# Last token group of a GLA + SwiGLU block: its operand differences moved from the seam into the SwiGLU stage

## The chip, the cores and the metric

The kernel runs on one NeuronCore of a Trainium2 chip. The metric is the device time of one execution in microseconds (us). The kernel before took 2386.27 us (median of three runs, 2382.10 to 2387.61).

## The reference

One layer: a modulated, normalised gated-linear-attention (GLA) mixer over 2048 latent tokens (256 context tokens only start its states), then a modulated, normalised SwiGLU feed-forward layer with F = 2816 hidden units, all in float32. With D = 1024, cut to what matters:

```python
h_lat = modulate(rms_norm(lat, norm_g[i, 0]), mod_l[:, 0], mod_l[:, 1])
y_lat, y_ctx = gla_mixer(h_lat, h_ctx, ...)
lat = lat + mod_l[:, 2] * rms_norm(y_lat, norm_g[i, 1])
h = modulate(rms_norm(lat, norm_g[i, 2]), mod_l[:, 3], mod_l[:, 4])
gate, up = jnp.split(h @ ffn_w_in[i], 2, axis=-1)
lat = lat + mod_l[:, 5] * rms_norm((silu(gate) * up) @ ffn_w_out[i], norm_g[i, 3])
```

## The kernel before, in words

Every float32 product is made of three TensorE (PE) matmuls in the fp32r type: an operand is split into a high part (a cast on ACT) and a low part (a subtraction on DVE), and hi x hi, hi x lo and lo x hi are added up in PSUM (`mm3`, `product`).

The 2048 tokens are four groups g = 0 to 3 of 512. The first stage projects the groups and runs the forward scan. The second (`back`, steps b0 to b4) goes through the sixteen 128-token tiles from the last to the first: inter-chunk part, head norm, gate, projection with `wout` (the `py` matmuls), residual and norm. b4 makes the tile `y` = l1 (the residual stream, stored to `l1_d`), and `norm_tile` its normalised copy `xh`.

The SwiGLU matmuls use a seven-product scheme on 2x2 blocks (Strassen-Winograd, P1 to P7) instead of eight products. Its four token-side blocks are the upper and lower half of the features k of two groups: groups 2 and 3 form the pair p = 1, groups 0 and 1 the pair p = 0. For each pair, seven operands `T_d[p][P1..P7]` are written to HBM: three are raw blocks of h (P1 = b11 and P2 = b21 from the odd group, P3 = b22 from the even one), four are differences. `h2_units(g)` makes them. For an odd group, `first(k)` transposes four `xh` tiles on PE (`tp`), evicts and modulates them on ACT (`hf`, line 103) and stores h. For an even group, `second(k)` loads back b11 and b21 of the odd group, makes b12 and b22, and computes four differences per k (`comb`, line 781), on POOL for g = 2 and on DVE for g = 0; each is stored by the SP queue.

The third stage works on the pair p = 1 first, then p = 0. `load_T` loads an operand (four tiles of 256 KB for k = 0 to 3, line 860) and splits it (cast line 861, subtraction line 862). `Feat` loads the weights of one 128-row feature block (`wg`, 512 KB, line 894; two `wu` of 256 KB, line 897). `product(i)` splits the weight block (`whl`: cast line 924, subtraction line 925) and issues 12 matmuls (line 942). There are 44 steps t of seven products; a step takes P1, P2, P6 and P7 of its own block and P5, P4 and P3 of the block before. Beside them run `w2_units`, one unit per step: loads of `w2` (tag `wl`), differences on DVE (line 878), stores on POOL's queue. The results are combined by DVE and stored by POOL (line 970). The fourth stage multiplies by `ffn_w_out`.

The order on each engine is set by the tile framework's scheduler from the written order, its cost estimates and the buffers; each engine and each queue then runs its list in order, and a DMA issue that waits holds everything behind it on its queue. Memory is given to pools as a stack from the left and one from the right; a tile of a new pool waits for the old tiles whose place it takes. At the seam between stages two and three, the code closes the pools of stage two, runs what is left of `h2_units(0)` (`pend`), opens the pools of stage three and loads the operands of pair 1 in the order P1, P2, P6, P7, P5, P4, P3, and only then the first weights.

Of the kernel before, what the change touches and what calls it, by code (L numbers as in the profile page):

```python
# [7 lines left out]
F32 = mybir.dt.float32  # L8
# [3 lines left out]
ALU = mybir.AluOpType  # L12
PSUM = bass.MemoryType.PSUM
# [21 lines left out]
def trunk(ctx, tc, x, cx, modw, cols, rows, consts, wqkr, wv, wvg, wgate, wout, w1, w2, out):  # L35
    nc = tc.nc
    sync = nc.sync
    st = nc.sync
# [8 lines left out]
    T_d = [[dram.tile([4, 128, GT], F32, name=f"T_d{p}{i}") for i in range(7)] for p in range(2)]  # L47
# [602 lines left out]
    def back(gc):  # L650
# [91 lines left out]
        def b4(xhs):  # L742
            y, ss2, pys = e["y"], e["ss2"], e["py"]
            xt = sq.tile([128, D], F32, name="xt2", tag="xt2", bufs=2)
            sync.dma_start(out=xt, in_=x[128 * gc:128 * gc + 128, :])
            sst = sq.tile([128, 1], F32, name="sst", tag="sst", bufs=2)
            nc.gpsimd.tensor_tensor(out=sst, in0=ss2[:, 0:1], in1=ss2[:, 1:2], op=ALU.add)
            rs = rstd_of(sq, sst, 1, float(D), "y")
            for n in range(2):
                ns = slice(512 * n, 512 * n + 512)  # L750
                nc.vector.scalar_tensor_tensor(out=y[:, ns], in0=pys[n], scalar=rs[:, 0:1], in1=A2[:, ns],
                                               op0=ALU.mult, op1=ALU.mult)
            (nc.vector if gc == 0 else nc.gpsimd).tensor_tensor(out=y, in0=y, in1=xt, op=ALU.add)  # L753
            st.dma_start(out=l1_d[gc], in_=y)
            xhs.append(norm_tile(sq, y, "b"))

        return [b0, b1, b2, b3, b4, rload]

    def h2_units(g, xhs):
        p, n1 = divmod(g, 2)  # L760
        Td = T_d[p]

        def hmod(k):
            hf = sq.tile([128, GT], F32, name="hf2", tag="hf2", bufs=4)
            transp_mod(ps2, "pa", 4, xhs, k, hf, mcol[:, 2, 1, k:k + 1], mcol[:, 2, 0, k:k + 1])
            return hf

        def first(k):
            st.dma_start(out=Td[P1 if k < 4 else P2][k % 4], in_=hmod(k))

        def second(k):
            eng = nc.gpsimd if g else nc.vector
            bl = sq.tile([128, D], F32, name="bl", tag="xt2", bufs=2)
            b11, b21 = bl[:, 0:GT], bl[:, GT:D]
            sync.dma_start(out=b11, in_=Td[P1][k])
            sync.dma_start(out=b21, in_=Td[P2][k])
            b12, b22 = hmod(k), hmod(k + 4)
            st.dma_start(out=Td[P3][k], in_=b22)

            def comb(i, out, x, y):  # L780
                eng.tensor_tensor(out=out, in0=x, in1=y, op=ALU.subtract)
# [39 lines left out]
    pend = []  # L821
# [20 lines left out]

    p3 = ExitStack()
    hL = p3.enter_context(tc.tile_pool(name="hL", bufs=1, reuse_waits="tile"))
    w3 = p3.enter_context(tc.tile_pool(name="w3", bufs=2, reuse_waits="tile"))
    o3 = p3.enter_context(tc.tile_pool(name="o3", bufs=2, reuse_waits="tile"))
    ps3 = p3.enter_context(tc.tile_pool(name="ps3", bufs=1, space=PSUM, reuse_waits="tile"))
    for u in pend:
        u()
    p2t.close()  # L850
    hR = p3.enter_context(tc.tile_pool(name="hR", bufs=1, reuse_waits="tile", side="right"))
    ps3z = p3.enter_context(tc.tile_pool(name="ps3z", bufs=1, space=PSUM, reuse_waits="tile", side="right"))
    T = {}

    def load_T(p, i):
        pool = hL if i in (P1, P2, P6) else hR
        t = pool.tile([128, 4, 2, GT], F32R, name=f"T{i}", tag=f"T{i}", bufs=1)
        for k in range(4):
            raw = t[:, k, 1, :].bitcast(F32)
            sync.dma_start(out=raw, in_=T_d[p][i][k])  # L860
            nc.scalar.copy(out=t[:, k, 0, :], in_=raw)  # L861
            nc.vector.tensor_sub(out=t[:, k, 1, :], in0=raw, in1=t[:, k, 0, :].bitcast(F32))
        T[i] = t

    def w2_units(fp):
        b = {}
# [18 lines left out]
    units = [u for fp in range(NFP) for u in w2_units(fp)]  # L885
    ins_of = lambda x: getattr(x, "ins", x)

    class Feat:


        def __init__(self, p, f):
            self.p, self.f = p, f
            self.wg = w3.tile([128, 1024], F32, name="wg", tag="wg", bufs=2)
            self.load = ins_of(sync.dma_start(out=self.wg, in_=w1[2 * f]))
            self.u = [w3.tile([128, 512], F32, name=f"wu{j}", tag=f"wu{j}", bufs=3) for j in range(2)]
# [295 lines left out]
```

## Time and profile before

| | before |
|---|---|
| median of three runs | 2386.27 us (2382.10 to 2387.61) |
| the profiled execution, its own time | 2380.79 us |
| its span in the profile | 2379.0 us |
| PE busy | 2300.5 us (97%) |
| DVE / ACT / POOL busy | 1560.5 (66%) / 1069.1 (45%) / 293.0 us (12%) |
| mean granted PE clock | 0.988 of full speed |
| PE idle inside 1078.6 to 1134.2 us (the seam) | 22.0 us |

The span is the time between the first and the last instruction that the profiler saw; the execution's own time is 1.8 us longer. Matmuls are pipelined: one takes 0.39 us from start to end, but the next starts 0.23 us later. The granted clock is 1.00 at 2.4 GHz and 0.50 at 1.2 GHz.

### The profile page before, as it was taken

To read this page: it belongs to the slowest core of one execution; us is meant where nothing else is said; L and a number is where in the kernel's file an instruction comes from. 1 tells how busy PE (TensorE), PEld (TensorE's weight loads), DVE (VectorE), ACT (ScalarE), POOL (GpSimd) and SP (SyncE) were. 2 spreads that over 40 slices of the span, in tenths; PEclk is the share of its full clock that TensorE was granted. 3 is DMA by queue.
4 is the path that set the end of the run, shared out by engine and by line. 5 is a ranking of instruction groups with operands and counts; after the bars stand their busy time and mean duration, and the time that the engine had idled before them with its cause. 6 is when DMAs were issued, how large, how long until landed. Compare 5 with 4: busy or idle time off the path is not lost.

```text
span 2379.0 us, 32495 instructions
## 1 busy us (share of the span) xinstructions
PE 2300.5 (97%) x11546; PEld 1938.3 (81%) x11546; DVE 1560.5 (66%) x2478; ACT 1069.1 (45%) x1947; POOL 293.0 (12%) x472
## 2 busy tenths in 40 slices
PE   7999999999998999896999999999999999999998
PEld 4898898898898878775888888888888888888886
DVE  5756666766659586657766666876666657466554
ACT  3525445445547544335433333533333336545552
POOL 1100000000001033631111111111111110011001
PEclk9999999999999999997999999999999999999999
DMA  8664468465455587759443333743344258569654
GB/s 297 224 212 169 150 199 291 168 215 203 153 190 197 201 281 251 245 180 319 156 137 132 133 124 134 240 153 126 129 135 140 102 170 287 194 198 326 198 187 159
DMA packets 213063, 458.22 MB, mean 193 GB/s; under 512 B 22178, under 2 KB 65826, under 8 KB 212900
## 3 DMA queue, kind: packets, MB, share of 16 engines
q1 hardware_dynamic: 197060, 404.23, 50.2%
q0 software_dynamic: 15840, 51.92, 6.0%
q8 instruction: 90, 1.47, 0.3%
q14 instruction: 73, 0.60, 0.1%
HBM read 325.50 MB, written 130.56 MB: 192 GB/s over the span
## 4 chain that ended last, share of the span: by engine, by line
PE 78%; DVE 7%; DMA 5%; issue 4%; POOL 3%; ACT 2%; SPq 0%; POOLq 0%; DVEq 0%; ACTq 0%
PE X L942 20%; PE X L1075 10%; PE Z L942 10%; PE W L1075 8%; PE pj L87 5%; PE pj L86 5%; PE pj L88 5%; PE Y L942 5%; PE o L494 1%; DMA xt<-modw 1%; POOL y L753 1%; PE sc L419 1%; DVE cs L335 1%; PE pj L287 1%; DVE wlo L76 1%
## 5 line engine op out<-in xcount | busy, mean ns | idle before, releaser
L942 PE MATMUL X<-T,whl 128*128 128x512 f32 x2112 | 497.6, 391 | 21.5 <-ACT whl L924 21.5
L942 PEld LDWEIGHTS X<-T,whl 128*128 128x128 f32 x2112 | 397.1, 188 | 105.8 <-ACT whl L924 23.2
L942 PE MATMUL Z<-T,whl 128*128 128x512 f32 x1056 | 254.5, 389 | 0.0
L1075 PE MATMUL X<-wr,ar 128*128 128x512 f32 x1056 | 240.9, 389 | 0.0
L942 PEld LDWEIGHTS Z<-T,whl 128*128 128x128 f32 x1056 | 198.3, 188 | 42.1 <-ACT T L861 0.7
L1075 PEld LDWEIGHTS X<-wr,ar 128*128 128x128 f32 x1056 | 198.2, 188 | 41.5
L86 PE MATMUL pj<-hhi,whi 128*128 128x512 f32 (+1 forms) x544 | 213.4, 395 | 2.1 <-DVE hhi L75 1.4
L87 PE MATMUL pj<-hlo,whi 128*128 128x512 f32 (+1 forms) x544 | 211.2, 389 | 0.0
L88 PE MATMUL pj<-hhi,wlo 128*128 128x512 f32 (+1 forms) x544 | 210.2, 387 | 0.0
L73 ACT CAST whi<-wf 128x1024 fp32r<-128x1024 f32 x104 | 109.0, 1048 | 190.8 <-PE pj L87 83.6
L1029 DVE TENSOR_TENSOR ar<-ar 128x512 fp32r<-128x512 f32 x154 | 106.0, 691 | 127.7 <-ACT ar L1028 126.9
L76 DVE TENSOR_TENSOR wlo<-wf,whi 128x1024 fp32r<-128x1024 f32 x104 | 126.8, 1220 | 86.2 <-ACT whi L73 80.5
L1075 PE MATMUL W<-wr,ar 128*128 128x512 f32 x792 | 180.8, 389 | 0.0
L1075 PEld LDWEIGHTS W<-wr,ar 128*128 128x128 f32 x792 | 148.7, 188 | 31.1
L1028 ACT CAST ar<-ar 128x512 fp32r<-128x512 f32 x154 | 95.5, 621 | 151.4 <-DMA ar<-S_d 106.4
L86 PE MATMUL pj<-whi,hhi 128*128 128x256 f32 x432 | 124.7, 289 | 6.1 <-DVE gs L292 4.9
L942 PE MATMUL Y<-T,whl 128*128 128x512 f32 x528 | 127.7, 390 | 0.0
L87 PE MATMUL pj<-wlo,hhi 128*128 128x256 f32 x432 | 123.3, 285 | 1.9 <-DVE wlo L76 1.9
L88 PE MATMUL pj<-whi,hlo 128*128 128x256 f32 x432 | 122.7, 284 | 0.0
L925 DVE TENSOR_TENSOR whl<-s,whl 128x512 fp32r<-128x512 f32 x132 | 90.7, 689 | 48.7 <-ACT whl L924 47.8
L87 PEld LDWEIGHTS pj<-hlo,whi 128*128 128x128 f32 x544 | 103.4, 190 | 21.2 <-DVE hlo L76 2.2
L86 PEld LDWEIGHTS pj<-hhi,whi 128*128 128x128 f32 x544 | 102.9, 190 | 21.2 <-DVE hhi L75 1.6
(234 smaller groups left out, 4391.2 us busy)
## 6 DMA issues: line engine op xcount, KB each, us to landing
ar<-S_d SPq DMA_DIRECT2D x154, 256.0 KB, 2.8
wf<-wqkr SPq DMA_DIRECT2D x68, 512.0 KB, 3.9
wg<-w SPq DMA_DIRECT2D x44, 512.0 KB, 3.8
wu<-w SPq DMA_DIRECT2D x88, 256.0 KB, 2.7
S_d<-sa POOLq DMA_DIRECT2D x88, 256.0 KB, 2.3
wr<-W_d SPq DMA_DIRECT2D x88, 256.0 KB, 2.9
wf<-wv SPq DMA_DIRECT2D x36, 512.0 KB, 3.9
S_d<-a POOLq DMA_DIRECT2D x66, 256.0 KB, 3.2
```

What stands on the lines that cost most here:

```text
L73: nc.scalar.copy(out=hi, in_=src)
L76: nc.vector.tensor_sub(out=lo, in0=src, in1=hi.bitcast(F32))
L86: nc.tensor.matmul(out=ps, lhsT=ahi, rhs=bhi, start=start, stop=False)
L87: nc.tensor.matmul(out=ps, lhsT=ahi, rhs=blo, start=False, stop=False)
L88: nc.tensor.matmul(out=ps, lhsT=alo, rhs=bhi, start=False, stop=stop)
L287: nc.tensor.matmul(out=ps[:, 0:n], lhsT=a, rhs=w[:, k % 4, 0:n], start=(k == 0 and j == 0), stop=(k == KT - 1 and j == 2))
L335: nc.vector.tensor_tensor_scan(out=flat(cs[:, 4 * hh:4 * hh + 4, :]), data0=flat(rst), data1=flat(gcs), initial=0.0, op0=ALU.mult, op1=ALU ...
L925: nc.vector.tensor_sub(out=w[:, 1, :], in0=src, in1=w[:, 0, :].bitcast(F32))
L942: nc.tensor.matmul(out=ps, lhsT=w[:, a, ks], rhs=t[:, k, b, :], start=first and k == 0 and n == 0, stop=k == 3 and n == 2, skip_group_chec ...
L1028: nc.scalar.copy(out=t[:, 0, :], in_=raw)
L1029: nc.vector.tensor_sub(out=t[:, 1, :], in0=raw, in1=t[:, 0, :].bitcast(F32))
L1075: nc.tensor.matmul(out=po[j], lhsT=a[:, x, 128 * j:128 * j + 128], rhs=w[:, z, :], start=first and fp == 0 and n == 0, stop=fp == NFP - 1 ...
```

## The change

Five edits. (1) Group 0 now also uses `first`: its eight h blocks are stored raw, b12 into the place of P7 and b22 into that of P3, by POOL's DMA queue instead of SP's. (2) The four differences per k for pair 0 are made by new units `t_units(k)` in the first eight steps of stage three: SP loads P7, P3, P1, P2 of one k into the `wl` buffers behind that step's `wg` load, in the next step POOL makes four subtractions and stores them by its own queue. The 44 `w2` units follow, and the last eight steps take two units each. (3) Pools: a new pool `c2o` holds `ohi`, `olo` of odd tiles; `c2b` moves under `sq`; operands P1, P2 (`hL`) and the weights (`wA`) come to lie over memory of `sp`; P6 (`hM`), P7 and P5 (`hE`), P4 and P3 (`hR`) lie over what is free later. (4) The operand P1, the first weights, and P2 are loaded before the rest of `pend`; the other operands after it; the third block's weights are held behind the last operand load. (5) The store of `l1_d[0]` goes to POOL's queue, behind `norm_tile`.

```diff
+    c2o = p2.enter_context(tc.tile_pool(name="c2o", bufs=1, reuse_waits="tile"))
...
-            p = c2 if gc % 2 else c2b
+            p = c2o if gc % 2 else c2b
...
-            st.dma_start(out=l1_d[gc], in_=y)
+            if gc:
+                st.dma_start(out=l1_d[gc], in_=y)
             xhs.append(norm_tile(sq, y, "b"))
+            if not gc:
+                nc.gpsimd.dma_start(out=l1_d[gc], in_=y)
...
         def first(k):
-            st.dma_start(out=Td[P1 if k < 4 else P2][k % 4], in_=hmod(k))
+            i = (P1 if k < 4 else P2) if n1 else (P7 if k < 4 else P3)
+            (st if g else nc.gpsimd).dma_start(out=Td[i][k % 4], in_=hmod(k))
...
-        if n1:
+        if n1 or g == 0:
             return [lambda k=k: first(k) for k in range(KT)]
...
+    c2b = p2t.enter_context(tc.tile_pool(name="c2b", bufs=1, reuse_waits="tile", side="right"))
     sq = p2t.enter_context(tc.tile_pool(name="sq", bufs=2, reuse_waits="tile", side="right"))
-    c2b = p2.enter_context(tc.tile_pool(name="c2b", bufs=1, reuse_waits="tile", side="right"))
...
+    def t_units(k):
+        b = {}
+        Td = T_d[0]
+
+        def load(sp_ins, dve_ins):
+            with tc.issue_after(sp_ins):
+                for i in (P7, P3, P1, P2):
+                    b[i] = o3.tile([128, 512], F32, name="wl", tag="wl", bufs=4)
+                    sync.dma_start(out=b[i], in_=Td[i][k])
+
+        def diff(i, out, x, y):
+            nc.gpsimd.tensor_tensor(out=b[out], in0=b[x], in1=b[y], op=ALU.subtract)
+            nc.gpsimd.dma_start(out=Td[i][k], in_=b[out])
+
+        def diffs(sp_ins, dve_ins):
+            diff(P5, P1, P7, P1)
+            diff(P7, P7, P3, P7)
+            diff(P6, P3, P3, P1)
+            diff(P4, P2, P2, P3)
+
+        return [load, diffs]
+
+    units = [u for k in range(4) for u in t_units(k)] + [u for fp in range(NFP) for u in w2_units(fp)]
...
-    for i in CHAIN:
-        load_T(1, i)
     n = len(seq)
+    load_T(1, P1)
+    feats[0] = Feat(*seq[0])
+    load_T(1, P2)
+    for u in pend:
+        u()
+    p2t.close()
...
+    last_T = [ins_of(load_T(1, i)) for i in CHAIN[2:]][-1]
     for t in range(n + 1):
-        if t < n:
+        if t == 2:
+            with tc.issue_after(last_T):
+                feats[t] = Feat(*seq[t])
+        elif 0 < t < n:
             feats[t] = Feat(*seq[t])
...
-        if units and t < n:
-            units.pop(0)(feats[t].load, feats[t].mark)
+        for _ in range(2 if t >= n - 8 else 1):
+            if units and t < n:
+                units.pop(0)(feats[t].load, feats[t].mark)
```

How it moves the lists of the engines. On PE at the seam, from the last `py` matmul on; the operands are P1 (T_10939 before, T_10826 now), P2 (T_10952, T_10845), P6 (T_10965, in the first list) and P7 (T_10953, in the second); `tp` are the transposes of group 0. Before:

```order
L88 MATMUL py<-wo_hi_8573,olo 128x512
L942 MATMUL X<-T_10939,whl 128x512 x2
L942 MATMUL Y<-T_10952,whl 128x512 x2
L942 MATMUL X<-T_10939,whl 128x512 x3
L102 MATMUL tp<-ident,xh 128x128 x24
L942 MATMUL X<-T_10939,whl 128x512 x4
L102 MATMUL tp<-ident,xh 128x128 x4
L942 MATMUL X<-T_10939,whl 128x512 x3
L942 MATMUL Y<-T_10952,whl 128x512 x3
L102 MATMUL tp<-ident,xh 128x128 x4
L942 MATMUL Y<-T_10952,whl 128x512 x7
L942 MATMUL X<-T_10965,whl 128x512 x12
```

Now:

```order
L88 MATMUL py<-wo_hi_8576,olo 128x512
L964 MATMUL X<-T_10826,whl 128x512 x12
L964 MATMUL Y<-T_10845,whl 128x512 x2
L102 MATMUL tp<-ident,xh 128x128 x32
L964 MATMUL Y<-T_10845,whl 128x512 x10
L964 MATMUL Z<-T_10953,whl 128x512 x2
L964 MATMUL X<-T_10826,whl 128x512 x2
L964 MATMUL Z<-T_10953,whl 128x512 x8
```

The same matmuls stand in a new order: all of P1 ahead of the transposes, and P7 of the first block right behind P2. From the third step on the two PE lists are the same.

On SP's DMA queue, from the last load of x on (T_d00, T_d01 are P1, P2 of pair 0; T_d02 to T_d06 its P3 to P7; T0_, T1_, T5_ operands P1, P2, P6 of pair 1). Before:

```order
L860 DMA T0_10939<-T_d10_85 128x512 x4
L860 DMA T1_10952<-T_d11_86 128x512
L769 DMA T_d01_79<-hf2_10696 128x512
L860 DMA T1_10952<-T_d11_86 128x512 x2
L769 DMA T_d01_79<-hf2_10704 128x512
L860 DMA T1_10952<-T_d11_86 128x512
L860 DMA T5_10965<-T_d15_90 128x512 x3
L754 DMA l1_d1_114<-y2_10622 128x1024
L775 DMA bl_10823<-T_d00_78 128x512
L776 DMA bl_10823<-T_d01_79 128x512
L860 DMA T5_10965<-T_d15_90 128x512
L894 DMA wg_11030<-w1 128x1024
```

Now:

```order
L859 DMA T0_10826<-T_d10_85 128x512 x4
L916 DMA wg_10839<-w1 128x1024
L774 DMA T_d01_79<-hf2_10699 128x512
L919 DMA wu0_10841<-w1 128x512
L774 DMA T_d01_79<-hf2_10707 128x512
L919 DMA wu1_10842<-w1 128x512
L859 DMA T1_10845<-T_d11_86 128x512 x3
L756 DMA l1_d1_114<-y2_10625 128x1024
L859 DMA T1_10845<-T_d11_86 128x512
L859 DMA T5_10940<-T_d15_90 128x512 x4
L859 DMA T6_10953<-T_d16_91 128x512 x4
L859 DMA T4_10966<-T_d14_89 128x512 x4
```

The first `wg` now stands right behind P1. Behind the rows shown, the list before has `wu` x2, four `wl` loads, the store of `l1_d[0]`, 6 more reloads of `bl` and 20 stores to T_d02 to T_d06 ahead of the second block's `wg`; now that `wg` follows at once, then the operands T3_ (P4) and T2_ (P3), of which T2_ waits for DMAs of POOL's queue, then the four `wl` loads of the first `t_units`.

On POOL, from the last `ry` on. Now (before, the rows of lines 759, 774, 896 and 897 are not there, and the `mb`, `rb` pair is followed by stores of W_d and S_d):

```order
L82 TENSOR_TENSOR ry_10795<-my_10793,nhalf_186 128x1
L759 DMA l1_d0_113<-y2_10735 128x1024
L80 TENSOR_SCALAR mb_10803<-ss_10801 128x1
L82 TENSOR_TENSOR rb_10805<-mb_10803,nhalf_186 128x1
L774 DMA T_d06_84<-hf2_10858 128x512
L774 DMA T_d06_84<-hf2_10866 128x512
L774 DMA T_d06_84<-hf2_10874 128x512
L774 DMA T_d06_84<-hf2_10882 128x512
L774 DMA T_d02_80<-hf2_10890 128x512
L774 DMA T_d02_80<-hf2_10898 128x512
L774 DMA T_d02_80<-hf2_10906 128x512
L774 DMA T_d02_80<-hf2_10914 128x512
```

Eight stores and the store of l1 came in; behind them stand four times (subtraction, store) for k = 0, then the first S_d store, and so on for k = 1 to 3.

## Rows read from the trace of the kernel before

**Rows 1.** The page's header and first part: busy time, share of the span and instructions of each engine.
```profile
span 2379.0 us, 32495 instructions
PE 2300.5 (97%) x11546; PEld 1938.3 (81%) x11546; DVE 1560.5 (66%) x2478; ACT 1069.1 (45%) x1947; POOL 293.0 (12%) x472
```

**Rows 2.** Busy time of PE, PEld, DVE, ACT and POOL (instructions in brackets) in stretches of the span, then granted clock, DMA share and GB/s: the seam, a quiet stretch of stage three, and its end.
```profile
1078.77:1134.21 55.44, 33.46 (x136) 25.68 (x135) 43.61 (x69) 30.78 (x56) 5.52 (x9) 0.75 0.90 316
...
1140.00:1150.00 10.00, 10.00 (x46) 8.29 (x45) 9.93 (x17) 4.88 (x10) 1.08 (x2) 1.00 0.64 212
1160.00:1200.00 40.00, 40.00 (x178) 33.13 (x177) 26.59 (x43) 14.95 (x26) 5.62 (x11) 1.00 0.35 122
...
1900.00:1960.00 60.00, 60.00 (x266) 49.71 (x265) 33.95 (x53) 21.58 (x39) 7.55 (x14) 1.00 0.48 161
```

**Rows 3.** PE in order of time at the seam: start, length, line, operation, in brackets the idle time ahead and what ended it.
```profile
1078.54 0.39 PE L88 MATMUL py<-wo_hi,olo 128*128 128x512 f32 x1
1087.20 1.22 PE L942 MATMUL X<-T,whl 128*128 128x512 f32 x2 [8.28 <-ACT whl L924]
...
1091.36 4.82 PE L102 MATMUL tp<-ident,xh 128*128 128x128 f32 x24 [0.52 <-DVE xh L95]
...
1100.84 2.89 PE L942 MATMUL X<-T,whl 128*128 128x512 f32 x12
1115.98 2.07 PE L942 MATMUL X<-T,whl 128*128 128x512 f32 x4 [12.25 <-ACT whl L924]
...
1126.06 2.88 PE L942 MATMUL Y<-T,whl 128*128 128x512 f32 x12
1128.78 2.88 PE L942 MATMUL Z<-T,whl 128*128 128x512 f32 x12
1132.59 1.26 PE L942 MATMUL X<-T,whl 128*128 128x512 f32 x4 [0.93 <-ACT whl L924]
1133.69 0.68 PE L942 MATMUL Z<-T,whl 128*128 128x512 f32 x2
```

**Rows 4.** The chain that ended last, at the seam: start, length, what.
```profile
1080.04 6.47 DMA wg<-w
...
1110.31 0.32 SPq L782
1110.68 4.62 DMA wg<-w
1115.31 0.63 ACT whl L924
```

**Rows 5.** The last tile's way from its second `py` half to the transposes, in order of time on ACT, POOL and DVE (three answers, merged by engine).
```profile
1081.47 0.59 ACT L739 ACTIVATE y<-py 128x512 f32<-128x512 f32 x1
...
1087.58 1.05 ACT L93 ACTIVATE xh<-y 128x1024 f32<-128x1024 f32 x1
...
1092.49 1.63 ACT L103 ACTIVATE hf<-tp,mcol 128x512 f32<-128x512 f32 x2 [3.77 <-PE tp L102]
...
1089.88 0.55 POOL L82 TENSOR_TENSOR rb<-mb,nhalf 128x1 f32<-128x1 f32 x1
...
1084.20 1.41 DVE L751 SCALAR_TENSOR_TENSOR y<-py,ry,A 128x512 f32<-128x512 f32 x2 [0.44 <-POOL ry L82]
...
1090.46 0.76 DVE L95 TENSOR_SCALAR xh<-y,rb 128x1024 f32<-128x1024 f32 x1 [0.72 <-POOL rb L82]
```

**Rows 6.** ACT: evictions of transposed tiles (min/median/max ns of one), and a row of three operand casts in order of time.
```profile
L103 ACT ACTIVATE hf<-tp,mcol x72: 547/776/791, 34.5 to 1105.9; 128x512 f32<-128x512 f32 x64, 128x256 f32<-128x256 f32 x8
...
1072.22 1.66 ACT L861 CAST T<-T 128x512 fp32r<-128x512 f32 x3
```

**Rows 7.** DMAs: stores on POOL's queue of stage three and operand loads on SP's (count, KB each, median us from issue to landing), and the extremes of line 970 and of line 860.
```profile
S_d<-a POOLq DMA_DIRECT2D x66, 256.0 KB, 3.2
T<-T_d SPq DMA_DIRECT2D x56, 256.0 KB, 4.7
...
L970 POOL DMA_DIRECT2D S_d<-a x66: 539/539/545, 1134.2 to 1950.7; - x66
DMA to landing us min/median/max: 2.3/2.3/7.4
...
L860 SPq DMA_DIRECT2D T<-T_d x56: 319/425/1367, 1060.6 to 1541.7; - x56
DMA to landing us min/median/max: 2.6/4.7/6.6
```

**Rows 8.** PE's busy time and granted clock in short stretches, and the pause ahead of one of them.
```profile
1012.90 1.48 PE L722 MATMUL tp<-ident,on 128*128 128x128 f32 x8 [2.52 <-DVE on L703]
...
1014.00:1016.00 2.00, 2.00 (x7) 0.50 1.00 259
1016.00:1018.00 2.00, 2.00 (x9) 0.75 0.52 155
```

**Rows 9.** POOL's differences of group 2 (min/median/max ns of one), and one POOL addition with the DVE subtraction that ran beside it, in order of time.
```profile
L781 POOL TENSOR_TENSOR hf<-hf,hf x4: 1267/1358/1629, 973.9 to 1000.9; 128x512 f32<-128x512 f32 x4
...
1075.02 2.77 POOL L753 TENSOR_TENSOR y<-y,xt 128x1024 f32<-128x1024 f32 x1 [1.52 <-DVE y L751]
...
1075.46 2.88 DVE L862 TENSOR_TENSOR T<-T 128x512 fp32r<-128x512 f32 x1
...
L862 DVE TENSOR_TENSOR T<-T x56: 677/682/2884, 1074.9 to 1547.8; 128x512 fp32r<-128x512 f32 x56
```

**Rows 10.** PE around the start of stage two, in two stretches of 10 us (busy columns and clock as in rows 2).
```profile
820.00:830.00 10.00, 8.53 (x39) 6.43 (x39) 7.72 (x15) 6.52 (x11) 1.76 (x2) 1.00 0.78 255
830.00:840.00 10.00, 8.15 (x41) 6.29 (x40) 6.73 (x16) 3.88 (x12) 1.21 (x2) 1.00 0.91 287
```

More of the change, by code (lines that the diff above doesn't have):

```diff
@@ L768, in first @@
         def first(k):
-            st.dma_start(out=Td[P1 if k < 4 else P2][k % 4], in_=hmod(k))
+            i = (P1 if k < 4 else P2) if n1 else (P7 if k < 4 else P3)
+            (st if g else nc.gpsimd).dma_start(out=Td[i][k % 4], in_=hmod(k))
         def second(k):
-            eng = nc.gpsimd if g else nc.vector
             bl = sq.tile([128, D], F32, name="bl", tag="xt2", bufs=2)
@@ L780, in comb @@
             def comb(i, out, x, y):
-                eng.tensor_tensor(out=out, in0=x, in1=y, op=ALU.subtract)
+                nc.gpsimd.tensor_tensor(out=out, in0=x, in1=y, op=ALU.subtract)
                 st.dma_start(out=Td[i][k], in_=out)
@@ L844, in trunk @@
     hL = p3.enter_context(tc.tile_pool(name="hL", bufs=1, reuse_waits="tile"))
+    wA = p3.enter_context(tc.tile_pool(name="wA", bufs=2, reuse_waits="tile"))
     w3 = p3.enter_context(tc.tile_pool(name="w3", bufs=2, reuse_waits="tile"))
-    o3 = p3.enter_context(tc.tile_pool(name="o3", bufs=2, reuse_waits="tile"))
     ps3 = p3.enter_context(tc.tile_pool(name="ps3", bufs=1, space=PSUM, reuse_waits="tile"))
[L848 to L852, printed above, removed]
     T = {}
     def load_T(p, i):
-        pool = hL if i in (P1, P2, P6) else hR
+        pool = hL if i in (P1, P2) else hM if i == P6 else hE if i in (P7, P5) else hR
         t = pool.tile([128, 4, 2, GT], F32R, name=f"T{i}", tag=f"T{i}", bufs=1)
@@ L859, in load_T @@
             raw = t[:, k, 1, :].bitcast(F32)
-            sync.dma_start(out=raw, in_=T_d[p][i][k])
+            loaded = sync.dma_start(out=raw, in_=T_d[p][i][k])
             nc.scalar.copy(out=t[:, k, 0, :], in_=raw)
@@ L863, in load_T @@
         T[i] = t
+        return loaded
     def w2_units(fp):
@@ L883, in w2_units @@
                 sums((P6, (0, 0), (0, 0), (1, 1), ALU.add)), sums((P4, (1, 0), (1, 0), (0, 0), ALU.subtract))]
-    units = [u for fp in range(NFP) for u in w2_units(fp)]
+    def t_units(k):
[16 more added lines that the diff above has]
+    units = [u for k in range(4) for u in t_units(k)] + [u for fp in range(NFP) for u in w2_units(fp)]
     ins_of = lambda x: getattr(x, "ins", x)
@@ L892, in __init__ @@
             self.p, self.f = p, f
-            self.wg = w3.tile([128, 1024], F32, name="wg", tag="wg", bufs=2)
+            self.wg = wA.tile([128, 1024], F32, name="wg", tag="wg", bufs=2)
             self.load = ins_of(sync.dma_start(out=self.wg, in_=w1[2 * f]))
-            self.u = [w3.tile([128, 512], F32, name=f"wu{j}", tag=f"wu{j}", bufs=3) for j in range(2)]
+            self.u = [wA.tile([128, 512], F32, name=f"wu{j}", tag=f"wu{j}", bufs=3) for j in range(2)]
             for j in range(2):
@@ L985, in trunk @@
     feats = {}
-    for i in CHAIN:
-        load_T(1, i)
     n = len(seq)
+    load_T(1, P1)
[4 more added lines that the diff above has]
+    p2t.close()
+    hM = p3.enter_context(tc.tile_pool(name="hM", bufs=1, reuse_waits="tile"))
+    o3 = p3.enter_context(tc.tile_pool(name="o3", bufs=2, reuse_waits="tile"))
+    hE = p3.enter_context(tc.tile_pool(name="hE", bufs=1, reuse_waits="tile", side="right"))
+    hR = p3.enter_context(tc.tile_pool(name="hR", bufs=1, reuse_waits="tile", side="right"))
+    ps3z = p3.enter_context(tc.tile_pool(name="ps3z", bufs=1, space=PSUM, reuse_waits="tile", side="right"))
+    last_T = [ins_of(load_T(1, i)) for i in CHAIN[2:]][-1]
     for t in range(n + 1):
-        if t < n:
+        if t == 2:
+            with tc.issue_after(last_T):
+                feats[t] = Feat(*seq[t])
+        elif 0 < t < n:
             feats[t] = Feat(*seq[t])
```

## The prediction

> **What bounds the kernel now.** I read four views in this order. The page's first part [rows 1] shows PE busy for 2300.5 of 2379.0 us: a change that leaves its matmuls as they are can only give back idle time. The table of stretches [rows 2] shows where that is: in stage three PE is busy without a break, at the full clock, while in the 55.4 us of the seam it works 33.5 us at a mean clock of 0.75. PE in order of time [rows 3] splits the seam's 22.0 idle us: 8.28 ahead of the first product, 0.52 ahead of the transposes, 12.25 ahead of the second feature block, 0.93 later. The chain [rows 4] names the cause of the two large ones. The first `wg` is issued at 1080.04 us, behind everything that SP's queue had to do for stage two, and takes 6.47 us to land; the second is issued at 1110.68, right behind the last of the 20 operand stores of group 0 (1110.31), and its cast starts at 1115.31. So the seam is bound by weights that come late because SP's queue holds them behind group 0's differences.
>
> **A ruler for the seam.** I measure from the end of the last `py` (1078.8) to the moment when 102 product matmuls and the 32 transposes are issued. Before, that is 1132.59 + 6 matmuls = 1134.2: 55.4 us. At the full clock a product matmul costs 0.227 us (12 of them from 1126.06 to 1128.78) [rows 3]. The 102 alone are 23.1 us.
>
> **The change, part by part.**
>
> *First weights and P1, P2 early.* Their loads now stand ahead of SP's wait for the `y` of tile 1, so the first `wg` lands before 1078.8 and its `whl` casts need only ACT, from about 1080.5. P1's matmuls start at about 1081 and wait once for DVE's low part (about 1083.8). This fills PE's wait for the last tile; it does not shorten it.
>
> *The last tile's way.* From Square (1081.47) over the two STTs (1084.20), the residual, the second Square (1087.58), `rb` (1089.88) and `xh` (1090.46) to the transposes at 1091.36 [rows 5]. ACT's list keeps as much ahead of that Square (three operand casts and two of `whl`, where five operand casts were), and DVE's about as much. I take 1091.4, as before. The `l1_d[0]` store now stands ahead of `mb` on POOL: one issue of 0.54 us [rows 7], covered by the Square of 1.05 us [rows 5] that `mb` waits for; without that cover it would cost 0.54.
>
> *Transposes and evictions.* All 32 transposes are now in one run, and what sets the end is ACT: eight evictions of 0.78 [rows 6] = 6.2, three operand casts between them of 0.55 (1.66 for three) [rows 6] = 1.7, and the casts of the next two `whl`, 1.1. From the first eviction at 1092.5 [rows 5] that gives 1101.5 for the next product, P7. The remaining matmuls of P2 run under it. The fifth eviction needs the first h store to have left its buffer: 1093.3 + 0.54 issue + 2.3 to 3.2 landing [rows 7] = 1096.1 to 1097.0, and ACT gets there at 1096.7. No term.
>
> *The rest without SP's differences.* The 16 DVE subtractions, 8 reloads and 20 stores are gone from the seam, so the second `wg` follows the operand loads and is there by about 1093. From 1101.5, 78 of the 102 are left: 78 x 0.227 = 17.7, so 1119.2.
>
> *The clock.* PE then pauses about 3 us (1098.8 to 1101.5). The nearest row is the pause of 2.52 us ahead of 1012.9: behind it the clock is 0.50 for 1014 to 1016 and 0.75 to 1018 [rows 8], some 3 us at half speed. Bounds: 0 and, with 3.2 us at half, 1.6. I take 1.6, since the pause is the longer one. 1120.8.
>
> *POOL's differences beside DVE.* A POOL subtraction of this size took 1.27 to 1.63 us [rows 9]. A DVE subtraction that started beside a POOL addition of 2.77 us lasted 2.88 instead of 0.68 [rows 9]: DVE stood until POOL was done. The first four differences fall at about 1111 to 1119, when DVE has to catch up. Bounds: 0 (DVE is ahead of PE) and 4 x 1.33 = 5.3 (all of it reaches PE). DVE ought to reach the next low part some 5 us before PE, so I take 1.0. 1121.8. For k = 1 to 3 DVE's spare time covers it: it is busy 26.6 of 40 us [rows 2], 12.7 of a step of 84 x 0.227 = 19.1, so 6.4 are free where 5.3 are needed; and no `w2` sums run in those steps.
>
> *Edits that cost nothing.* The eight steps that `w2` units start later are made up by two units in each of the last eight; DVE has 26 of 60 us free there [rows 2]. Pair 0's operands are ready by about 1200, and their last load stands at 1541.7 [rows 7]. `c2o` and `c2b` change some waits of the `wout` loads at the start of stage two; PE idles 3.3 us in those 20 us [rows 10], so at most that much could go or be added again. I take 0, PE's list is unchanged there.
>
> **Sum.** 1134.2 - 1121.8 = 12.4 us less, and PE runs without a break behind it, so nothing gives it back. The profiled execution took 2380.8 (span 2379.0 and 1.8 around it), and would take 2368.4; it is 5.5 below the median of the runs, 2386.3, which I use: 2386.3 - 12.4 = **2373.9**.
>
> **The rivals.**
>
> *More is given back.* If P7's casts don't wait for the evictions, P7 starts when P2 ends, at 1098.8, without a pause, a slower clock or a DVE wait: 1098.8 + 17.7 = 1116.5, 17.7 us less, 2368.6. For it: PE and DVE have the time. Against it: in ACT's list both casts stand behind the eighth eviction.
>
> *A new wait on SP.* The operand P3 lies over the h buffers, so its load waits for the h stores of POOL's queue, and behind it on SP stand the `wl` loads and the third block's weights. The last eviction ends at about 1100.4; with 0.54 issue and 2.3 to 7.4 landing [rows 7] the load is issued at 1103 to 1108, four loads are there 5 to 7 us later [rows 7], and ACT's and DVE's in-order lists have them ahead of a low part that PE wants at 1117.8. That is 3 to 8 us of slack. If the stores need 8 us more than the slack, 8 of the 12.4 are lost: 2382, within the noise. For it: POOL's queue is new in this place and the DMA share of the seam is 0.90 [rows 2].
>
> *DVE becomes the bound, and the kernel slower.* If DVE stands still for all sixteen differences, 16 x 1.33 = 21.3 us, and has no time to spare in the first four steps, PE is late by all of it: 13.4 (the gain without the DVE term) - 21.3 = 7.9 us more, 2394.2. It decides where DVE's free time per step falls below 5.3 us. For it: DVE is busy 9.93 of 10 us just behind the seam, at 1140 to 1150 [rows 2]; against it: only 26.6 of 40 from 1160 on. The Trainium skill (SBUF — State Buffer, "Who interferes with whom") says that a DVE instruction with two SBUF inputs and a GpSimd one that reads SBUF exclude each other for the whole instruction. The 2.88 us agree with that, and the rule speaks against putting these sums on POOL beside a DVE that is short of time. By the rule alone, where every difference costs DVE its full length, the sum would be this rival's when DVE is the bound, and the forecast's when it is not.
>
> **How the numbers follow.** Forecast 0.71, more given back 0.15, the wait on SP 0.10, slower 0.04. A measurement of this kernel can tell some 0.2%, 4.8 us, from no change. Faster: 0.71 + 0.15 = 0.86; same 0.10; slower 0.04. The forecast's own bounds are 8 us less (5.3 for DVE in place of 1.0) to 15 (no slower clock, no DVE wait), 2371 to 2378; with a spread of the runs of 2.7 either way and the first rival, the range is 2367 to 2381.
>
> **What would show it.** Right: PE issues P1's 12 matmuls and then waits for the transposes at about 1091; no wait for a `wg` is left; P7 starts at 1100 to 1103 behind ACT's casts; the idle time in the seam is about 12 us in place of 22; SP shows one wait, for the h stores, with no PE wait behind it; POOL's differences lie between 1110 and 1200. Wrong: PE idle behind 1105 for a `whl` that DVE or a weight load holds up; DVE subtractions of over 1.3 us in series with PE waiting; or a first transpose later than 1093.

## The result, and the profile after

| | before | after |
|---|---|---|
| median of the runs, same chip | 2384.61 us | 2367.83 us (2366.31 to 2369.52) |
| profiled execution, span | 2380.79, 2379.0 us | 2366.31, 2364.5 us |

The ratio is 0.9932, with a 95% interval from 0.992 to 0.9944: 16.8 us less by the medians. The forecast was 2373.9 in a range from 2367 to 2381, so the time is in the range, near its low end. The forecast is 6.1 us too long: its gain of 12.4 us was too small by 4.4, and the kernel before, put at 2386.27, has a median of 2384.61 here. The two profiled executions say where the gain lies:

| part of the span | before | after | difference |
|---|---|---|---|
| start to the last `py` (PE's instructions unchanged) | 1078.8 | 1081.6 | +2.8 |
| the ruler: to 102 product matmuls and the 32 transposes | 55.4 | 39.9 | -15.5 |
| from there to the last matmul | 1234.4 | 1235.8 | +1.3 |
| last matmul to the end of the span | 10.3 | 7.2 | -3.1 |

The first row is variation: over all kernels below, the same PE instructions took from 1078.2 to 1085.4 us. Without it the sum is -17.3, beside the -16.8 of the medians.

The page's first part, after:
```profile
PE 2301.9 (97%) x11546; PEld 1940.2 (82%) x11546; DVE 1566.6 (66%) x2462; ACT 1066.5 (45%) x1947; POOL 328.4 (14%) x513
```
Beside [rows 1], PE has the same work and 14.5 us less of span around it. DVE has sixteen instructions less and is busy for 6.1 us more: that belongs to POOL's differences, further down.

Stretches of the span after; columns as in [rows 2]. The first is the ruler, the second what follows P7's start, the third the place where [rows 2] showed DVE without time to spare.
```profile
1081.55:1121.48 39.93, 31.99 (x135) 25.73 (x135) 35.18 (x52) 29.36 (x55) 14.32 (x21) 0.87 0.90 312
...
1103.60:1121.50 17.90, 17.88 (x79) 14.69 (x80) 17.09 (x24) 11.16 (x21) 4.26 (x5) 1.00 0.83 285
1140.00:1150.00 10.00, 8.88 (x40) 7.03 (x39) 9.97 (x13) 4.21 (x8) 4.84 (x7) 1.00 0.72 244
```
PE after, in order of time at the seam and at the fourth step; columns as in [rows 3].
```profile
1083.91 0.73 PE L964 MATMUL X<-T,whl 128*128 128x512 f32 x2 [2.13 <-ACT whl L946]
1086.61 4.64 PE L964 MATMUL X<-T,whl 128*128 128x512 f32 x10 [1.97 <-DVE whl L947]
...
1094.17 5.35 PE L102 MATMUL tp<-ident,xh 128*128 128x128 f32 x32 [2.07 <-DVE xh L95]
1099.28 2.57 PE L964 MATMUL Y<-T,whl 128*128 128x512 f32 x10
1103.62 0.74 PE L964 MATMUL Z<-T,whl 128*128 128x512 f32 x2 [1.76 <-ACT whl L946]
...
1120.12 2.20 PE L964 MATMUL X<-T,whl 128*128 128x512 f32 x9
...
1143.17 3.01 PE L964 MATMUL X<-T,whl 128*128 128x512 f32 x12 [1.12 <-DVE a L979]
```
Of the two large waits of [rows 3], 8.28 and 12.25 us, none is left; the idle time in the ruler is 2.13 + 1.97 + 2.07 + 1.76 = 7.9 us. No wait ends at a `wg` any more, because the first was issued at 1065.88 and the second at 1089.20 (SP's queue after):
```profile
1065.88 0.41 SPq L916 DMA_DIRECT2D wg<-w  x1
...
1080.99 7.86 SPq L859 DMA_DIRECT2D T<-T_d  x13
1089.20 0.33 SPq L916 DMA_DIRECT2D wg<-w  x1
...
1099.56 10.68 SPq L859 DMA_DIRECT2D T<-T_d  x8
```
What sets P7's start (the first Z, 1103.62) is ACT, whose rows run without a gap but one from the first eviction to the `whl` casts:
```profile
1094.84 2.78 ACT L103 ACTIVATE hf<-tp,mcol 128x512 f32<-128x512 f32 x4 [0.93 <-PE tp L102]
1097.50 1.15 ACT L860 CAST T<-T 128x512 fp32r<-128x512 f32 x2
1099.24 2.12 ACT L103 ACTIVATE hf<-tp,mcol 128x512 f32<-128x512 f32 x3 [0.59 <-DMA T_d<-hf]
1101.24 0.62 ACT L860 CAST T<-T 128x512 fp32r<-128x512 f32 x1
1101.75 0.79 ACT L103 ACTIVATE hf<-tp,mcol 128x512 f32<-128x512 f32 x1
1102.42 1.14 ACT L946 CAST whl<-s 128x512 fp32r<-128x512 f32 x2
```
POOL's first differences, and DVE's rows beside them:
```profile
1118.76 1.31 POOL L896 TENSOR_TENSOR wl<-wl 128x512 f32<-128x512 f32 x1
...
1120.94 1.30 POOL L896 TENSOR_TENSOR wl<-wl 128x512 f32<-128x512 f32 x1
```
```profile
1116.20 0.68 DVE L979 TENSOR_TENSOR a<-a,X 128x512 f32<-128x512 f32 x1
1116.80 1.63 DVE L949 TENSOR_TENSOR s<-wg,s 128x512 f32<-128x512 f32 x1
1118.36 4.45 DVE L947 TENSOR_TENSOR whl<-s,whl 128x512 fp32r<-128x512 f32 x2
```
The two DVE subtractions at 1118.36 took 4.45 us where two alone take 1.3. That is DVE standing still beside POOL (the run with the differences on DVE, below, bears this out). From 1140 to 1150 it is busy for 9.97 of 10 us, and at 1143.17 PE has to wait for it once, for 1.12.

### The profile page after: what moved, and what is told of

Its sections match the earlier page's. It is cut to its first block, busy times and chain, and to the rows that moved or that the text cites. A ratio compares the mean times of both kernels' runs of the same rounds, so it can differ in the third digit from the quotient of the medians.

```text
span 2364.5 us, 32530 instructions
## 1 busy us (share of the span) xinstructions
PE 2301.9 (97%) x11546; PEld 1940.2 (82%) x11546; DVE 1566.6 (66%) x2462; ACT 1066.5 (45%) x1947; POOL 328.4 (14%) x513
## 4 chain that ended last, share of the span: by engine, by line
PE 75%; DVE 8%; DMA 6%; issue 5%; POOL 3%; ACT 3%; SPq 0%; POOLq 0%; DVEq 0%; ACTq 0%
PE X L964 19%; PE X L1111 10%; PE Z L964 10%; PE W L1111 8%; PE Y L964 5%; PE pj L87 5%; PE pj L86 5%; PE pj L88 5%; DMA xt<-modw 2%; POOL y L754 1%; PE o L494 1%; DMA xt<-x 1%; DVE cs L335 1%; PE sc L419 1%; PE pj L287 1%
## 5 line engine op out<-in xcount | busy, mean ns | idle before, releaser
L947 DVE TENSOR_TENSOR whl<-s,whl 128x512 fp32r<-128x512 f32 x132 | 98.2, 746 | 47.3 <-ACT whl L946 46.5
```

The source lines that it names most:

```text
L947: nc.vector.tensor_sub(out=w[:, 1, :], in0=src, in1=w[:, 0, :].bitcast(F32))
```

## The experiments

Theory after the result: SP's in-order queue held weights and operands behind group 0's differences; with these gone, the last tile's way and ACT's list set the seam. Rival: early loads and raw `h` each remove one of the two waits, and the gains add. All rulers and ends below are read as in the table above, from one profiled execution each; each time stands beside the median of the kernel before that was measured together with it.

**Early loads alone (e1).** The other half of the change is undone in the whole change's kernel (the differences go back to DVE in the seam, all stores to SP):
```diff
-        if n1 or g == 0:
+        if n1:
             return [lambda k=k: first(k) for k in range(KT)]
...
-    units = [u for k in range(4) for u in t_units(k)] + [u for fp ...
+    units = [u for fp ...
```


> Only the early loads and the new pools: group 0's differences are made in the seam as before (4 x 4 DVE subtractions, 20 stores and 8 reloads on SP). Ruler: last py end to 102 product matmuls and 32 transposes issued; before 55.4 us, with the whole change 39.9. Theory (SP's queue holds the second block's weights behind the 20 stores; the 8.28 us ahead of the first product lie under the last tile's way and are worth nothing by themselves): the second wg now stands behind the stores (31.5 us after the last py), 13 operand loads (8.7 us by 10.73 for 16) and four wl loads (1.6), is issued at about +42 and lands at +47 to +49; 54 products of 0.227 us are left then: ruler +61, 5 to 7 us slower than before, 2390 to 2392. Rival (each early load removes its own wait, whatever happens to the stores): 8.3 us faster, 2376.

Measured: 2389.57 us against 2385.69, ratio 1.0018 (1.0009 to 1.0027): slower. PE waits 2.13 us ahead of the first product, later 4.95 and 4.71 in P7, and then 10.80 for the second block; ruler 63.1. The medians are 3.9 us apart, the rulers of the two profiles 7.7. PE, and SP at the place:
```profile
1081.64 0.73 PE L960 MATMUL X<-T,whl 128*128 128x512 f32 x2 [2.13 <-ACT whl L942]
...
1128.11 7.67 PE L960 MATMUL X<-T,whl 128*128 128x512 f32 x24 [10.80 <-ACT whl L942]
```
```profile
1109.77 1.28 SPq L782 DMA_DIRECT2D T_d<-bl  x1
1111.10 7.24 SPq L855 DMA_DIRECT2D T<-T_d  x13
1118.69 2.36 SPq L868 DMA_DIRECT2D wl<-w  x4
1121.41 0.33 SPq L912 DMA_DIRECT2D wg<-w  x1
```
The wait of 8.28 us was worth little by itself: without it the first transpose comes 11.95 us behind the last `py`, in place of 12.6. The rival falls. The loss comes mainly from the second block's weights, which stand behind 13 operand loads here and are issued at +42, in place of +32.

**Early loads for two blocks (e8).** As above, with one line more ahead of the operand loads: `feats[1] = Feat(*seq[1])`.

> As e1, but the weights of the second block are loaded ahead of group 0's stores too. Theory: the weights no longer bound the seam, and the operands do: the load of P6's last quarter and all 16 of P7, P5, P4, P3 stand behind the 20 stores (issued from +32 on, 0.67 us each), so P7 starts at about +39 with 54 products left: ruler 51 to 54 us, 1.5 to 4 us less than before, 2380 to 2383. Rival (late weights alone were the cost): the ruler comes down to the 40 us of the whole change, 2369.

Measured: 2381.8 against 2385.69, ratio 0.9978 (0.9969 to 0.9987); ruler 51.0, so 4.4 less than before. The weights are there, and PE waits twice behind the transposes; PE, then ACT:
```profile
1108.97 4.21 PE L960 MATMUL X<-T,whl 128*128 128x512 f32 x9 [8.85 <-ACT g L964]
1116.46 0.55 PE L960 MATMUL X<-T,whl 128*128 128x512 f32 x1 [3.28 <-ACT T L856]
```
```profile
1105.04 1.66 ACT L942 CAST whl<-s 128x512 fp32r<-128x512 f32 x3 [3.76 <-DVE s L931]
...
1108.35 1.06 ACT L964 COPY g<-X 128x512 f32<-128x512 f32 x2
```
So it is not the weights' place alone. The 3.28 us are for an operand, whose load stands behind the stores on SP. The 8.85 are not: PE waits there for ACT to copy the first product (`g`), and in ACT's list that copy stands behind two evictions of group 0 and a cast that waited 3.76 us for DVE, which was busy for 19.05 of the 19.2 us from 1093.8 on, with group 0's sixteen differences among its work. So the differences in the seam seem to cost time on these two engines too, not on SP's queue alone; no run separates the two.

**Raw h alone (e2).** The kernel before, with only the raw stores and the store of `l1_d[0]` on POOL's queue and the later differences:
```diff
-            st.dma_start(out=Td[P1 if k < 4 else P2][k % 4], in_=hmod(k))
+            i = (P1 if k < 4 else P2) if n1 else (P7 if k < 4 else P3)
+            (st if g else nc.gpsimd).dma_start(out=Td[i][k % 4], in_=hmod(k))
...
```


> Only the raw h: group 0's h is stored as it is on POOL's queue, the differences are made later by POOL from reloads; operands, weights and pools stay where they were before. Theory (the stores on SP were the cost): the first wg is issued at about the same time as before, so PE still waits 6 to 8 us ahead of the first product, under the last tile's way; the second wg follows it at once, and the wait of 12.25 us is gone; P7's operand lies over the h buffers, its load is issued at about +26, and PE waits 2 to 4 us for it at about +30: ruler 43 to 46 us, 9.5 to 12.5 us less than before, 2372 to 2375. Rival (each half of the change removes one of the two waits and the gains add): 15.5 - 8.3 = 7.2 us faster, 2377.5. Other rival (the early half does nothing): all of the 15.5, 2369.

Measured: 2374.07 against 2385.69, ratio 0.9949 (0.9933 to 0.9965); ruler 47.2, so 8.2 less there, a little short of the theory's 9.5, and 3.1 less at the end (below). PE still waits for the first product, and for P7's operand as expected:
```profile
1091.02 1.22 PE L968 MATMUL X<-T,whl 128*128 128x512 f32 x2 [5.44 <-ACT whl L950]
...
1118.17 0.79 PE L968 MATMUL Z<-T,whl 128*128 128x512 f32 x1 [4.53 <-ACT T L865]
```
Its 16 operand loads are issued from 1111.95, 26.5 us behind the last `py`. The halves together bring 15.5 in the ruler, alone 8.2 and -7.7: the early loads, as the whole change has them, pay only once the differences are out of the seam, and then 7.3 us.

**h stores on SP (e3).** `st.dma_start(...)` in place of `(st if g else nc.gpsimd).dma_start(...)` in `first`.

> The whole change, but the eight h stores of group 0 on SP's queue instead of POOL's (they stand there behind the second wg and 12 of the early operand loads, ahead of the loads of P4 and P3). Theory (it was the differences and what stood behind them, not the queue, that cost time): the fifth eviction's wait of 0.59 us goes or stays, ruler 39 to 41, time within 2 us of the whole change. Rival (SP's waits for the evictions hold the second block's wu and the last operands): P6 or P4 of the second block late, PE waits 3 us or more behind +33, 2371 or more.

Measured: 2370.56 against 2386.96, ratio 0.9939 (0.9925 to 0.9952), where the whole change had 0.9934 beside it. No wait over 0.61 us behind P7's start, at +22.45. In the seam the queue does not matter for these eight stores, since weights and the early operands are ahead of them. The Trainium skill (Trainium Kernel Development and Optimization, "Key Constraints") says that issuing DMAs from several engines only saves issue time. As far as the seam goes this run agrees, with the two ratios above. The ruler is 41.8 here, and the clock makes 1.5 of the difference. The end is 11.8 in place of 7.2 (see the end of the program); the medians, 0.9 apart, don't show these 4.5 us, so whether the queue matters for the time stays open. PE, and its stretch behind the pause:
```profile
1096.69 2.56 PE L964 MATMUL Y<-T,whl 128*128 128x512 f32 x10
1101.69 1.22 PE L964 MATMUL Z<-T,whl 128*128 128x512 f32 x2 [2.44 <-ACT whl L946]
```
```profile
1101.60:1106.30 4.70, 4.61 (x13) 3.69 (x14) 4.59 (x8) 2.60 (x6) 0.00 (x0) 0.64 0.96 282
```

**Differences on DVE (e4).** `nc.vector` in place of `nc.gpsimd` in `diff`.

> The whole change, but the sixteen differences are made by DVE instead of POOL, from the same reloads. Theory (DVE pays for a POOL subtraction anyway, by standing still): 16 x 0.68 = 10.9 us more work for DVE against standing times of about 16 x 0.6 to 1.0; the wait of 1.12 us at step 4 goes or stays below 2.5, time within 2 us of the whole change apart from the end. Rival a (POOL's work is free for DVE): DVE is late by up to 0.68 x 4 per 20 us behind the seam, PE waits 3 us or more, 2371 or more. The end of the program: if its 3.1 us hang on DVE's list (2478 instructions again) it is 10.3 and the time 3.1 us longer; if they hang on SP's list, 7.2.

Measured: 2370.2 against 2386.96, ratio 0.9928 (0.9914 to 0.9941): the same as the whole change. No PE wait for DVE is left behind the seam, and DVE's busy time fell from 1566.6 to 1560.1 us although it does sixteen instructions more:
```profile
L896 DVE TENSOR_TENSOR wl<-wl x16: 678/684/693, 1121.7 to 1176.0; 128x512 f32<-128x512 f32 x16
```
Sixteen of 0.68 are 10.9 us; with the 6.5 that it saves, DVE had stood still for 17.4, some 1.1 us for each POOL difference of 1.30. The rival (POOL's work is free for DVE) falls. The end is 7.3, so it does not hang on DVE's list.

**POOL's work doubled (e7).** Ahead of each difference, POOL makes it once more in two halves into a scratch tile.

> The whole change, with POOL's work doubled: ahead of each of the sixteen differences POOL makes the same one in two halves into a scratch tile that nobody reads. Theory (DVE stands while POOL subtracts, has little to spare at 1140 to 1160 and 6.4 us per step behind that): the wait for DVE of 1.12 us at 1143 grows by 2 to 6 us, 2370 to 2374. Rival a (DVE is ahead of PE and hides it): no change from the 2367.8 of the whole change. Rival b (all of DVE's standing time reaches PE): 16 x 1.33 = 21 us more, 2389.

Measured: 2376.57 against 2385.69, ratio 0.9956 (0.9941 to 0.9972): 8.7 above the whole change by the medians, which were not measured together, and 5.7 by the two ratios to the kernel before (0.9956 and 0.9932); so that it is more than the theory's 2 to 6 is not shown. PE, and the stretch behind its wait:
```profile
1180.99 2.88 PE L967 MATMUL X<-T,whl 128*128 128x512 f32 x12
1189.40 5.49 PE L967 MATMUL X<-T,whl 128*128 128x512 f32 x12 [5.53 <-DVE a L982]
```
```profile
1189.40:1194.80 5.40, 5.40 (x13) 4.24 (x14) 5.40 (x7) 2.14 (x4) 5.22 (x6) 0.50 0.56 183
```
The wait grew from 1.12 to 5.53 as expected; behind it the clock was 0.50 and twelve matmuls took 5.49 in place of 2.88. Together 4.4 + 2.6 = 7.0: this wait of PE cost its own length and the slow clock behind it. The ruler is 41.9, 2 us more, but that is no effect of the doubling: e3, e4 and e6 have it without.

**Evictions shared with DVE (e5).** Every second eviction of group 0 as `nc.vector.tensor_scalar(out=dst, in0=tp, scalar1=sc, scalar2=sh, ...)`.

> The whole change, but every second one of group 0's eight evictions is made by DVE (scale and add from PSUM) instead of ACT. Theory (ACT's evictions and casts set P7's start): ACT has four evictions of 0.7 to 0.78 us less ahead of P7's cast, the pause of 1.76 us ahead of P7 goes, ruler 38.2, 1.8 us less, 2366. Rival (DVE, busy 4.3 to 5.0 of every 5 us there, becomes late with P7's low part instead): PE waits for DVE's whl there, ruler 40 or more, no gain.

Measured: 2367.61 against 2386.96, ratio 0.9921 (0.9908 to 0.9934), not to be told from the whole change. The ruler is 43.6: DVE's eviction at 1098.92 stands ahead of P2's low part, and PE waits for that:
```profile
1098.92 0.80 DVE L104 TENSOR_SCALAR hf<-tp,mcol 128x512 f32<-128x512 f32 x1
1099.64 0.68 DVE L951 TENSOR_TENSOR whl<-wg,whl 128x512 fp32r<-128x512 f32 x1
```
```profile
1100.38 3.94 PE L968 MATMUL Y<-T,whl 128*128 128x512 f32 x10 [3.11 <-DVE whl L951]
```
The rival was right, but for the place: it is P2's low part that comes late, not P7's. From the last `py` to the last matmul it takes 1277.8 us, some 2 more than the whole change (1275.5 and 1276.2), since there is no wait for DVE at the fourth step to make up for the 3.7; a median cannot show 2 us here.

**Differences later (e6).** Eight `w2` units stand ahead of them: `units = wu[:8] + [t_units ...] + wu[8:]`.

> The whole change, but the sixteen POOL differences and their reloads stand behind the first eight units of w2 in the list of units, so they fall outside the first steps behind the seam. Theory (the wait of 1.1 to 1.4 us for DVE at step 4 comes from POOL's differences beside a busy DVE): the wait goes, ruler 40 to 41.6 as in the four runs of this layout, last py to last matmul 1274.5 to 1276.5, time 1.2 us less or the same as the whole change. Rival (DVE is short of time there by itself, or w2's sums take the differences' place): the wait stays at 1 us or more.

Measured: 2364.19 against 2386.23, ratio 0.9909 (0.9894 to 0.9924). The wait at the fourth step is gone, as the theory wants. The ruler is 41.9, and last `py` to last matmul takes 1276.1, against 1275.5 and 1276.2 in the two profiles of the whole change; so this profile shows no gain to go with the median, and the intervals of the ratios overlap. A gain over the whole change is likely, not shown.

**Both (e10).** The former, and only the last two evictions on DVE.

> e6, and the last two of group 0's eight evictions on DVE (every second one was too many: P2's low part stood behind them). Theory (ACT sets P7's start; a pause of 2.2 us or more ahead of it costs 1.5 us more through the clock): P7 starts 1.4 us earlier, at 20.7 us behind the last py, the pause shrinks to below 1 us, the granted clock behind it stays 1.00, ruler 38.5; no wait at step 4: 2.5 us less than the whole change, 2365 to 2367. Rival (DVE cannot take them in time): P7's or P6's low part is late, ruler 40 or more, no gain.

Measured: 2365.2 against 2386.23, ratio 0.9907 (0.9894 to 0.9921). P7 starts at +20.8 behind a pause of 0.79, at the full clock, as the theory has it; then the rival takes the gain, a wait of 1.53 for P7's second low part, and the ruler is 40.5:
```profile
1102.55 0.73 PE L969 MATMUL Z<-T,whl 128*128 128x512 f32 x2 [0.79 <-ACT whl L951]
1103.11 0.69 PE L969 MATMUL X<-T,whl 128*128 128x512 f32 x2
1105.33 2.11 PE L969 MATMUL Z<-T,whl 128*128 128x512 f32 x8 [1.53 <-DVE whl L952]
```
Relieving ACT hands the bound to DVE within 1.5 us.

**The end of the program.** Three runs ask where the 3.1 us came from. The first (after_again) is the whole change once more:

> The whole change once more, beside the runs of this call. 2367 to 2369. Ruler 39.9 us, last matmul to the end of the span 7.2 (10.3 in the kernel before): in the five kernels looked at so far this end is 10.3 where DVE has 2478 instructions and SP's list some 1012 rows, and 7.2 to 7.7 where they have 2462 and some 997. Theory: it belongs to the program, and stays 7.2. Rival: it is chance from run to run, and may be 10.3 here.

Measured: 2369.64 against 2386.96, ratio 0.9934 (0.992 to 0.9948); end 7.2 once more, ruler 40.3. So the end belongs to the program.

Then (e9) the whole change with eight small loads more on SP's queue, `sync.dma_start(out=cc, in_=cols[:, 0:4])` in steps 20 to 27:

> The whole change with eight loads of 2 KB more on SP's queue, which nobody reads, in the first steps of SwiGLU. The end (last matmul to the end of the span) was 10.3 us in the three kernels with 1184 DMAs on SP's list, 11.8 in the one with 1179 and 7.2 to 7.7 in the five with some 1171; DVE's list does not go with it. Theory (it hangs on SP's list alone): with 1179 the end is 10 to 12 us and the time some 3 to 4.5 us above that of the whole change, 2371 to 2373. Rival (it hangs on something else in those kernels): 7.2 to 7.7, no change of the time.

Measured: 2367.75 against 2386.23, ratio 0.9917 (0.9904 to 0.9931); end 7.3. SP's list falls as a cause. Its profile has the longest ruler of this seam, 43.3: the last eviction waits 1.71 us for an `h` store to leave its buffer, PE pauses 4.31 ahead of P7, and the clock behind it is 0.54:
```profile
1105.00 0.78 ACT L103 ACTIVATE hf<-tp,mcol 128x512 f32<-128x512 f32 x1 [1.71 <-DMA T_d<-hf]
```

Last (e12) the kernel before, with the first 25 stores to `W_d` made twice on POOL's queue:
```diff
                     nc.gpsimd.dma_start(out=W_d[i][fp], in_=b[out])
+                    if len(nx) < 25:
+                        nc.gpsimd.dma_start(out=W_x[len(nx)], in_=b[out])
+                        nx.append(1)
```


> The kernel before, with 25 more stores of 256 KB on POOL's queue in SwiGLU (the first 25 of the stores to W_d are made a second time, into a tensor that nobody reads): 223 DMAs there, as the whole change has, in place of 198. The end (last matmul to the end of the span) was 10.3 us in the three kernels with 198 DMAs on POOL's queue, 11.8 in the one with 215 and 7.2 to 7.7 in all eight profiles with 223. Theory (it hangs on what POOL's queue has handled): 7.2 to 7.7, the rest as before, so the time is about 3 us less than before, 2382 to 2384. Rival (it hangs on something else that the kernels with 223 share): 10.3, no change.

Measured: 2382.84 against 2385.23, ratio 0.9987 (0.9977 to 0.9996). The ruler is 56.4, 1.0 above that of the kernel before, the end 7.0. The last DVE instruction of the whole change and then of this kernel:
```profile
2359.26 1.28 DVE L1092 SCALAR_TENSOR_TENSOR y<-y,rz,l 128x1024 f32<-128x1024 f32 x1 [0.49 <-POOL rz L82]
```
```profile
2376.96 1.28 DVE L1062 SCALAR_TENSOR_TENSOR y<-y,rz,l 128x1024 f32<-128x1024 f32 x1 [0.49 <-POOL rz L82]
```
From there to the end of the spans, 2364.5 and 2381.9, are 4.0 and 3.7 us; in the kernel before the same instruction ends at 2371.95 and the span at 2379.0, 7.05 later. So with 25 more DMAs on POOL's queue, in two kernels that have them in different places, the end is about 3 us shorter.

The traces show what fills it. At its end the program has a DRAIN on POOL; the longest of three, in ns, in the kernel before, the whole change, e3 and e12:
```profile
L1187 POOLq DRAIN  x3: 40/102/8196, 2370.0 to 2378.8; - x3
```
```profile
L1223 POOLq DRAIN  x3: 40/93/1579, 2358.6 to 2364.3; - x3
```
```profile
L1223 POOLq DRAIN  x3: 40/93/9584, 2357.7 to 2367.8; - x3
```
```profile
L1193 POOLq DRAIN  x3: 40/102/1579, 2376.3 to 2381.7; - x3
```
In the kernel before it runs from 2370.04 to 2378.24, 0.8 us before the end, when the last store to `out_dram` (issued at 2371.98, there 2.6 us later) has long landed. In the whole change it is over at 2360.2, and the end waits for that store, issued at 2360.57 and there 2.6 us later, 1.3 before the end. Why the DRAIN's length goes with the number of DMAs is open: 198 gave 8.2 us (end 10.3), 215 gave 9.6 (11.8), 223 gave 1.6 (7.0 to 7.7), so it is not simply fewer or more.

## Why the prediction was right, and where its sizes were off

The way was right: the wait for the second block's weights behind group 0's stores was the cost, no `wg` ends a wait now, P7 starts behind ACT's casts, and no operand is late. What it gave no price to is the time that group 0's differences may cost through DVE and ACT (e8). The terms:

- **Last tile's way, 12.6.** Measured 12.6 (1081.6 to 1094.17), and 12.56 to 12.59 in every kernel with the whole change's seam. It is what bounds the first half of the seam now.
- **Transposes to P7, 10.1.** Measured 9.45 in this profile, and 9.83 to 10.79 in the six others of this seam, so the size was sound. The first eviction started 0.67 behind the first transpose, not 1.1; eight cost 5.7 in their rows, not 6.2. "No term" for the wait on the `h` stores holds for four of the seven; here the fifth eviction waited 0.59 for the first store, on the path (0.23 in e4), and in e9 the eighth 1.71.
- **78 matmuls, 17.7.** Measured 17.86.
- **Clock, 1.6.** The price was right, and the two profiles of the whole change were spared it: here the pause was 1.76 us in place of 2.7, since P7 was ready 0.65 earlier and P2's rest ended 0.3 later than I put them, and the granted clock behind it was 1.00. In the kernels where the pause was 2.23 to 2.45 (e3, e4, e6 and e7) the same 78 matmuls took 19.4, so 1.5 more, and 19.9 in e9. The slow clock under the transposes (0.67 from 1094.1 to 1099.3) cost nothing here, as it fell into ACT's time; in the second profile it was 0.50, and the first eviction came 0.45 later.
- **DVE beside POOL, 1.0.** The size was right, the place was not: nothing in the ruler, 1.12 at the fourth step (1.40 in the second profile). The Trainium skill (SBUF — State Buffer, "Who interferes with whom") has a DVE instruction with two SBUF inputs and a GpSimd one that reads SBUF shut each other out. The trace agrees: two DVE subtractions lasted 4.45 us beside two of POOL, and over all sixteen DVE stood 1.1 us for each POOL difference of 1.30. The rival built on that rule did not come, but at twice POOL's work DVE's reserve was gone.
- **The end, unchanged.** Wrong by 3.1 us. I took what lies around the last matmul as given. It goes with the number of DMAs that POOL's queue issues, through the DRAIN on POOL; that the end was POOL's DRAIN stood in the trace of before, that it would shrink did not. These 3.1 us are no part of the mechanism: e12 has them from 25 stores that do no useful work.

Together: 12.4 + 0.65 (P7 earlier) + 1.4 (clock) + 1.0 (DVE) = 15.5 in the ruler; less 1.3 behind it, and 3.1 at the end, 17.3. The first rival's 2368.6 is close to the measured time, but not its mechanism: P7's casts did wait for the evictions. The seven profiles with this seam have rulers from 39.9 to 43.3, with a mean of 41.6, where the forecast put 55.4 - 12.4 = 43.0. So it is partly luck that the profile of the whole change lies so far below the forecast's ruler, and the 3.1 us of the end are the surest part of the error.

## What to carry to other kernels

Follow an in-order DMA queue as one follows an engine: a store that waits for its data delays every load behind it, and removing an earlier wait gains little while that store still stands there. Of two waits in a row, price the second first: the early loads of one block were worth -7.7 us in the ruler with the stores in the queue and 7.3 without them. Then look for the next in line: with both blocks' weights ahead of the stores (4.4 us), an operand and ACT's list were late. Work given to POOL beside a DVE with two-input instructions is not free, and here DVE would have made the differences for less than it stood still.

## What was not expected of the hardware

- Ahead of P7, a pause of PE of 0.79 to 1.76 us left the granted clock at 1.00, and one of 2.23 to 2.45 was followed by 0.64 to 0.68 in the next 5 us (e3, e4, e7). The length of the pause alone does not tell: ahead of the transposes a pause of 2.07 was followed by 0.67 in the whole change, one of 2.08 by 1.00 in e9:
```profile
1096.06:1101.06 5.00, 4.97 (x37) 4.29 (x38) 5.00 (x9) 4.33 (x7) 2.24 (x4) 1.00 0.87 327
```
- The time from the last matmul to the end of the span changed by 3 to 4.5 us with the number of DMAs that POOL's queue had issued, in kernels that end with the same instructions: the DRAIN on POOL took 1.6, 8.2 or 9.6 us.
- The same instructions ahead of the seam took from 1078.2 to 1085.4 us from one execution to the next, which is more than several of the effects looked for; parts of a span were therefore compared, not whole spans.
